# Feeding x transposed and applying its norm afterwards, in a one-core encoder block

## The chip, the cores and the metric

One core of a Trainium2 chip. The metric is the device time of one launch in microseconds (us), as the median of several runs; a separate profiled execution leaves a trace. PE is TensorE, DVE is VectorE, ACT is ScalarE, POOL is GpSimd, and SP is the engine whose queue issues nearly all loads.

## The reference

One layer over S = 256 tokens and D = 1024 channels. Cut to what matters here:

```python
xn = rms_norm(x, norm1_g)             # x * rsqrt(mean(x*x) + eps) * g, a factor per token and a gain per channel
a_x, a_g, b_q, ..., d_g, gate_logits = split(xn @ w_in)
y_a = rglru(a_x, a_g, ...)            # conv over time, gates, a linear recurrence both ways, times gelu(a_g)
y_b = diff_attention(b_q, b_k, b_v)
y_c = mla(c_q, c_kv, c_kpe)
y_d = retention(d_q, d_k, d_v, d_g)   # head layer norm of the result, times silu(d_g)
gates = sigmoid(gate_logits + gate_b)
merged = sum(gates[i] * (y_i @ w_br_i))
x = x + merged @ w_out
...                                   # feed-forward and a gated projection
```

Since rms_norm's factor is one number per token, `xn @ w` is the same as `(x * g) @ w` with each token's row multiplied by its factor.

## The kernel before

Every matrix product is made of three: weights and activations are split into a rounded part `hi` and a rest `lo`, and hi*hi, hi*lo and lo*hi are added in PSUM. `split` and `pieces` do this: ACT copies to `hi` (line 196), DVE subtracts for `lo` (line 190). For the pieces counted in `V_HI` with an even number, DVE makes `hi` too. Weights arrive in loads of up to 1 MB (`load`, line 372, three buffers `raw`), in the order in which they are used. `b_mode` (weights stationary, 256 columns out, one chunk = one load = 48 products) serves the recurrence branch and its gate; `a_mode` (activations stationary, up to 512 columns) the rest.

At the start x comes in as rows (four loads), each row tile's factor is computed (`rstd`: ACT's Square with a sum, a Sqrt, DVE's reciprocal), DVE multiplies, PE transposes 16 tiles, and `split_scaled` (lines 220 and 221) writes `xT` in hi and lo with the gain. Then four chunks `a_in(u)` follow, each evicted by a convolution of four taps on ACT and DVE (tile `xc`). `derived_params` runs behind the first: small parameter work, mostly DVE (`rg`, `lamp`, `spt`, `sp`).

Beside this main stream of products, generators do the branches' inner work: `a_mix` (the recurrence), `b_rot` and `b_mix` (attention), `c_mix`, `d_rot` and `d_mix`. `start` puts one on a list, and `tick`, called behind each chunk, lets it advance by a credit. A scheduler then lays out each engine's instructions in one fixed order; `tc.high_priority` moves some ahead. Each engine runs its list in order, so one that waits holds up what is behind it. The tile names in the trace: `raw` loaded weights, `hi` and `lo` their parts, `acc` and `mm` PSUM banks, `xs` x (later the merged sum), `par` the small parameters, `bd` the recurrence's gate weights, `bT` the attention's queries and keys, `y` the branches' results.

Of the kernel before, what the change touches and what calls it, by code (L numbers as in the profile page):

```python
# [26 lines left out]

V_HI = range(8, 40)

# [129 lines left out]
def _pack(w):  # L159
    import numpy as np  # L160

    return {'x': np.asarray(w['x']), 'weights': _pack_weights(w), 'params': _pack_params(w), 'lru': _pack_lru(w),
            'pT': np.ascontiguousarray(np.asarray(w['p'])[0, 0].T.reshape(2, P, S).transpose(1, 0, 2)),
            'gate_b': np.ascontiguousarray(np.asarray(w['gate_b'])[0]), 'decay': _decay()}


@with_exitstack
def encoder_kernel(ctx: ExitStack, tc: tile.TileContext, a, out):
# [55 lines left out]

    xs = const.tile([P, 2, D], F32, name="xs")
    par = const.tile([P, N_PAR], F32, name="par")
    with tc.high_priority(FIRST):
        for t in range(2):
            for c in range(2):
                w = slice(512 * c, 512 * c + 512)  # L230
                nc.sync.dma_start(xs[:, t, w], a['x'][0, t * P:(t + 1) * P, w])  # L231
        nc.sync.dma_start(par[:, :O_LATE], a['params'][:, :O_LATE])

# [5 lines left out]

    act(eps[:, 2:3], eps[:, 0:1], AF.Sqrt)  # L240
    nhalf = const.tile([P, 16], F32, name="nhalf")
# [5 lines left out]
    rope = par[:, O_ROPE:].rearrange("p (t w) -> p t w", t=2)  # L247
    rg = const.tile([P, 2, 2, 2, 80], F32, name="rg")
    lams = const.tile([P, 4], F32, name="lams")
# [4 lines left out]

    def derived_params():
        nc.sync.dma_start(par[:, O_LATE:], a['params'][:, O_LATE:])
# [8 lines left out]
        lamp = const.tile([P, 2, 64], F32, name="lamp")  # L265
        tt(lamp, lv[:, :, 0, :], lv[:, :, 1, :], MULT)
# [3 lines left out]

        nc.vector.tensor_scalar(out=gng, in0=c1('ret_gn_g'), scalar1=0.5, scalar2=None, op0=MULT)
        nc.vector.tensor_scalar(out=subg, in0=c1('diff_sub_g'), scalar1=1.0 - LAM_INIT, scalar2=None, op0=MULT)


        lamc = par[:, _COL['lru_lambda']:_COL['lru_lambda'] + 16]
        spt = const.tile([P, 4, 16], F32, name="spt")
        y_, s_, z_, q_ = (spt[:, j, :] for j in range(4))
# [151 lines left out]
    def b_mode(xh, xl, name, n0):  # L429

        ps = acc_bank().rearrange("p (f s) -> p f s", s=S)
        raw = load(name, 0, n0)
        for f in range(2):
            hi, lo = pieces(raw, f * 1024, 1024)
            for k in range(8):
                w = slice(k * P, (k + 1) * P)
                mm(ps[:, f, :], hi[:, w], xh(k), k == 0, False)
                mm(ps[:, f, :], hi[:, w], xl(k), False, False)
                mm(ps[:, f, :], lo[:, w], xh(k), False, k == 7)
        tick(1)  # L440
        return ps

    def b_wide(name, n0):
# [12 lines left out]
        return ps  # L456

    W_in = 'w_in'
    xh = lambda k: xTh[:, k, :]
    xl = lambda k: xTl[:, k, :]  # L460

    with tc.tile_pool(name="br", bufs=1) as br:
# [4 lines left out]
        def SH(name):  # L467
            return br.tile([P, 512], F32, tag="SH", name=name, bufs=NS)

        with tc.high_priority(FIRST):  # L470
            for t in range(2):
                r_ = rstd(xs[:, t, :], lambda: SH("xsq"))
                nc.vector.tensor_scalar(out=xs[:, t, :], in0=xs[:, t, :], scalar1=r_, scalar2=None, op0=MULT)
            for k2 in range(4):
                pt = mm_bank().rearrange("p (k s) -> p k s", s=S)
                for t in range(2):
                    for k in range(2):
                        kk = 2 * k2 + k
                        transpose(pt[:, k, t * P:(t + 1) * P], xs[:, t, kk * P:(kk + 1) * P])
                for k in range(2):  # L480
                    kk = 2 * k2 + k
                    split_scaled(xTh[:, kk, :], xTl[:, kk, :], pt[:, k, :], c1('norm1_g', kk))

# [242 lines left out]
        def c_in():  # L726

            cs = [L("cs").rearrange("p (t c) -> p t c", t=2) for _ in range(3)]
            for c0, n0, nn in ((0, O_CQ, 384), (384, O_CKV, 320)):
                ps = a_full(xh, xl, W_in, 8, n0, nn)  # L730
                for t in range(2):
                    for lo in range(0, 704, 256):
                        u0, u1 = max(lo, c0), min(lo + 256, c0 + nn)
                        if u0 < u1:
                            act(cs[lo // 256][:, t, u0 - lo:u1 - lo], ps[t][:, u0 - c0:u1 - c0], AF.Copy)
            return cs
# [135 lines left out]
        def d_in():  # L872

            res = [[], []]
            for j, o0 in enumerate((O_DQ, O_DK)):
                ps = a_full(xh, xl, W_in, 8, o0, 512)
                for c in range(2):
                    x = SH("dx").rearrange("p (t c) -> p t c", t=2)
                    for t in range(2):
                        act(x[:, t, :], ps[t][:, 256 * c:256 * c + 256], AF.Copy)  # L880
                    dst = [L("dqk", F32R).rearrange("p (h s) -> p h s", s=S) for _ in range(2)]
# [16 lines left out]
        def d_vg(c):  # L898
# [3 lines left out]
            for p in range(2):  # L902
                v = L("dv").rearrange("p (t c) -> p t c", t=2)
                for t in range(2):
                    act(v[:, t], ps[t][:, 256 * p:256 * p + 256], AF.Copy)
                pairs[p].append(v.rearrange("p t (h e) -> p t h e", e=P))
            ps = a_full(xh, xl, W_in, 8, O_DG + 512 * c, 512)
            for p in range(2):
                sg = L("dsg").rearrange("p (t c) -> p t c", t=2)
                for t in range(2):  # L910
                    pv = ps[t][:, 256 * p:256 * p + 256]
                    act(sg[:, t], pv, AF.Tanh, scale=0.5)
                    stt(sg[:, t], sg[:, t], 1.0, pv, ADD, MULT)
# [3 lines left out]
        def d_mix(p, qT, kT, v, sg, yy):  # L917
# [51 lines left out]
        for u in range(4):  # L969
            xc = a_in(u)  # L970
            if u == 0:
                derived_params()
# [159 lines left out]
```

## Time and profile before

| | |
|---|---|
| median of 3 runs | 727.56 us (726.92 to 728.64) |
| profiled execution | 728.43 us, of which the span of the trace is 726.6 us |
| PE busy | 711.9 us of the span |
| DVE, ACT, POOL busy | 535.9, 437.9 and 47.1 us |
| loads | 128.45 MB, 177 GB/s over the span |

A row of the timeline gives start, length, engine, line, operation and tiles (written `out<-in`); the brackets at its end give the idle time ahead of it and who ended that. In a row of waits stand the total, the number and the longest. A busy PE is not PE at its peak; the pace of its products is read from the starts.

### The profile page before, as it was taken

How to read it: one execution, taken by the hardware profiler on the slowest of the kernel's cores; microseconds unless marked ns; L12 is line 12 of the kernel's file. 1: busy time of each engine (PE TensorE's matmuls, PEld its weight loads, DVE VectorE, ACT ScalarE, POOL GpSimd, SP SyncE). 2: the span in 40 equal slices, each digit the busy share in tenths (PEclk: the TensorE clock that was granted, in tenths of full speed). 3: DMA queues.
4: the chain of work that ended last, by engine and by line, in shares of the span. 5: the costliest groups of instructions: out<-in, count | busy, mean ns of one | idle time of the engine just before them, and what ended most of it. 6: DMA issues, size and time to landing. Idle time of an engine off the chain costs nothing.

```text
span 726.6 us, 10163 instructions
## 1 busy us (share of the span) xinstructions
PE 711.9 (98%) x3810; PEld 607.6 (84%) x3810; DVE 535.9 (74%) x931; ACT 437.9 (60%) x770; POOL 47.1 (6%) x58
## 2 busy tenths in 40 slices
PE   5999999999999999999999999999999999999997
PEld 4988889998888888888888888888888888888876
DVE  5988978888777878967667588776788887445652
ACT  7589858585755994765655434545855555445551
POOL 0000003212011022200000012000000000000000
PEclk9999999999999999999999999999999999999999
DMA  8754554365344256355436583554565455536611
GB/s 304 261 225 169 179 174 142 117 222 214 133 162 137 93 175 230 120 186 175 138 125 233 199 281 126 179 197 144 182 223 176 174 182 203 195 124 233 230 57 53
DMA packets 22801, 128.45 MB, mean 177 GB/s; under 512 B 2656, under 2 KB 2912, under 8 KB 9440
## 3 DMA queue, kind: packets, MB, share of 16 engines
q1 hardware_dynamic: 22752, 127.80, 49.9%
q8 instruction: 30, 0.49, 0.3%
q14 instruction: 19, 0.16, 0.1%
HBM read 126.74 MB, written 1.05 MB: 176 GB/s over the span
## 4 chain that ended last, share of the span: by engine, by line
PE 88%; DVE 5%; ACT 2%; DMA 2%; POOL 1%; issue 1%; SPq 0%; ACTq 0%; DVEq 0%
PE acc L199 66%; PE acc L203 12%; PE mm L199 5%; PE mm L212 3%; DVE lo L190 2%; DMA raw<-in_weights_dram 2%; PE mm L203 1%; ACT hi L196 1%; ACT be L196 1%; DVE bsm L675 0%; DVE xT L193 0%; POOL bss L296 0%; POOL crq L296 0%; POOL crk L296 0%; SPq L231 0%
## 5 line engine op out<-in xcount | busy, mean ns | idle before, releaser
L190 DVE TENSOR_TENSOR lo<-raw,hi 128x1024 fp32r<-128x1024 f32 (+3 forms) x226 | 268.5, 1194 | 104.0 <-ACT hi L196 103.4
L196 ACT ACTIVATE hi<-raw 128x1024 fp32r<-128x1024 f32 (+3 forms) x210 | 217.1, 1040 | 194.0 <-PE acc L199 148.0
L199 PE MATMUL acc<-hi,xT 128*128 128x512 f32 (+3 forms) x752 | 233.4, 385 | 0.0
L199 PEld LDWEIGHTS acc<-hi,xT 128*128 128x128 f32 x752 | 139.5, 188 | 25.9
L199 PE MATMUL acc<-hi,y 128*128 128x512 f32 x448 | 142.7, 393 | 0.0
L199 PE MATMUL acc<-lo,xT 128*128 128x512 f32 (+3 forms) x376 | 142.6, 379 | 0.0
L199 PEld LDWEIGHTS acc<-hi,y 128*128 128x128 f32 x448 | 84.1, 188 | 18.0 <-ACT y L196 0.3
L203 PE MATMUL acc<-xT,hi 128*128 128x512 f32 x256 | 90.4, 399 | 0.0
L199 PE MATMUL acc<-lo,y 128*128 128x512 f32 x224 | 87.4, 391 | 0.0
L199 PEld LDWEIGHTS acc<-lo,xT 128*128 128x128 f32 x376 | 70.8, 188 | 12.1
L203 PE MATMUL acc<-xT,lo 128*128 128x256 f32 x256 | 71.6, 281 | 0.0
L203 PEld LDWEIGHTS acc<-xT,hi 128*128 128x128 f32 x256 | 48.1, 188 | 12.1
L199 PEld LDWEIGHTS acc<-lo,y 128*128 128x128 f32 x224 | 42.1, 188 | 8.2
L203 PEld LDWEIGHTS acc<-xT,lo 128*128 128x128 f32 x256 | 48.4, 189 | 0.1
L199 PE MATMUL acc<-xT,hi 128*128 128x256 f32 x256 | 47.7, 287 | 0.4 <-ACT xT L196 0.2
L199 PEld LDWEIGHTS acc<-xT,hi 128*128 128x128 f32 x256 | 40.4, 193 | 1.0 <-DVE xT L193 0.6
L199 PE MATMUL acc<-hi,h 128*128 128x512 f32 x128 | 40.8, 398 | 0.0
L199 PE MATMUL acc<-xT,lo 128*128 128x256 f32 x128 | 36.2, 284 | 0.3 <-DVE lo L190 0.3
L199 PEld LDWEIGHTS acc<-hi,h 128*128 128x128 f32 x128 | 24.0, 188 | 5.7
L199 PE MATMUL acc<-lo,h 128*128 128x512 f32 x64 | 25.3, 396 | 0.0
L199 PEld LDWEIGHTS acc<-xT,lo 128*128 128x128 f32 x128 | 24.5, 192 | 0.6 <-DVE lo L190 0.6
L199 PE MATMUL acc<-hi,cT 128*128 128x384 f32 (+1 forms) x80 | 24.2, 369 | 0.3 <-ACT cqp L196 0.3
(224 smaller groups left out, 896.2 us busy)
## 6 DMA issues: line engine op xcount, KB each, us to landing
raw<-in_weights_dram SPq DMA_DIRECT2D x104, 1024.0 KB, 4.8
raw<-in_weights_dram SPq DMA_DIRECT2D x6, 512.0 KB, 3.5
raw<-in_weights_dram SPq DMA_DIRECT2D x4, 576.0 KB, 3.8
bd<-in_lru_dram SPq DMA_DIRECT2D x8, 256.0 KB, 5.3
gb<-in_gate_b_dram SPq DMA_DIRECT2D x8, 256.0 KB, 5.3
dec<-in_decay_dram SPq DMA_DIRECT2D x8, 256.0 KB, 6.2
raw<-in_weights_dram SPq DMA_DIRECT2D x2, 768.0 KB, 4.5
raw<-in_weights_dram SPq DMA_DIRECT2D x2, 640.0 KB, 3.6
```

The source lines that it names most:

```text
L190: nc.vector.tensor_tensor(out=o, in0=x, in1=y, op=op)
L196: nc.scalar.activation(o, x, f, **kw)
L199: nc.tensor.matmul(o, lhsT=lhsT, rhs=rhs, start=start, stop=stop)
L203: nc.tensor.matmul(o, lhsT=lhsT, rhs=rhs, start=start, stop=stop, skip_group_check=True)
L212: nc.tensor.transpose(o, x, ident[:x.shape[0], :x.shape[0]])
```

## The change

x is given a second time, transposed and with norm1's gain in front (`xT`), and loaded in four parts, each followed by a quarter of the first chunk's weights in runs of 1 KB. `x_split` scales by the gain and splits straight from the loaded data, unnormalized. The rows of x are loaded behind the third chunk's weights (`xr`) and used only for the tokens' factors: `x_stats` gives `rc` (a factor per token, tokens on partitions), its half `rch`, and `rT` (the same along the free dimension, through two small products). Who reads a product applies the factor: DVE multiplies by `rT` for the recurrence branch (tiles `xa` and `gel`), ACT's copies take `rc` as their scale, the gates' addition becomes a multiply and add, and retention's values get it behind their norm on POOL. The first chunk has an order of its own in `b_mode`, and loads of the first three chunks are issued first. Eight products of zeros open PE's list. `rg` and two small scalings go from DVE to POOL. `V_HI` is narrower. `a_mix` of the first three chunks is started behind the third chunk.

```diff
-V_HI = range(8, 40)
+V_HI = range(16, 32)
+WARM = 8
...
+    with tc.high_priority(2 * FIRST):
+        nc.scalar.dma_start(par[:, 8:O_LATE], a['params'][:, 8:O_LATE])
+        for u in range(3):
...
+            if u:
+                nc.sync.dma_start(raw, src.rearrange("(p c) -> p c", c=2048))
+                continue
...
+            for k in range(0, 8, 2):
+                o0, o1 = 8 + S * k if k else 0, 8 + S * (k + 2)
+                nc.sync.dma_start(xs_[:, o0:o1], a['xT'][:, o0:o1])
+                w = slice(P * k, P * (k + 2))
+                nc.sync.dma_start(raw0v[:, :, w], src[:, :, w])
...
+        for _ in range(WARM):
+            mm(pt[:, 0:P], cold, cold, True, True)
...
-                    tt(rg[:, j, cs, :, o:o + w], rope[:, :, r0:r0 + w], g, MULT)
+                    nc.gpsimd.tensor_tensor(out=rg[:, j, cs, :, o:o + w], in0=rope[:, :, r0:r0 + w], in1=g, op=MULT)
...
+                    with tc.high_priority(FIRST):
+                        if k0 + k2 == 0:
+                            nc.vector.tensor_copy(out=hv[:, :, w], in_=rw)
+                        else:
+                            act(hv[:, :, w], rw, AF.Copy)
+                        x_split(k0 + k2)
+                        tt(lv[:, :, w], rw, hv[:, :, w].bitcast(F32), SUB)
+                        x_split(k0 + k2 + 1)
...
+    def x_split(k):
+        split_scaled(xTh[:, k, :], xTl[:, k, :], xin[:, k, :], xs_[:, k:k + 1])
+
+    def x_stats():
+        st = small.tile([P, 2, 2], F32, tag="xst", name="xst", bufs=1)
+        for t in range(2):
+            for c in range(2):
+                act(xr[2 * t + c], xr[2 * t + c], AF.Square, accum_out=st[:, t, c:c + 1])
+        tt(rc, st[:, :, 0], st[:, :, 1], ADD)
+        act(rc, rc, AF.Sqrt, scale=1.0 / D, bias=eps[:, 0:1])
+        nc.vector.reciprocal(rc, rc)
+        nc.vector.tensor_scalar(out=rch, in0=rc, scalar1=0.5, scalar2=None, op0=MULT)
+        pr = mm_bank()
+        for t in range(2):
+            mm(pr[:, t * P:(t + 1) * P], rc[:, t:t + 1].to_broadcast([P, P]), ident, True, True)
+        act(rT, pr[:, :S], AF.Copy)
...
-                tt(g, ps, gb, ADD)
+                stt(g, ps, rc[:, t:t + 1], gb, MULT, ADD)
...
-            ps = b_mode(xh, xl, W_in, O_AX + u * 256)
+            pp = b_mode(xh, xl, W_in, O_AX + u * 256)
+            if u == 0:
+                x_stats()
+            ps = SH("xa").rearrange("p (f s) -> p f s", s=S)
+            tt(ps, pp, rT.unsqueeze(1).to_broadcast([P, 2, S]), MULT)
...
-            act(gel, ps, AF.Gelu_apprx_tanh)
+            tt(gel, ps, rT.unsqueeze(1).to_broadcast([P, 2, S]), MULT)
+            act(gel, gel, AF.Gelu_apprx_tanh)
...
-                        act(x[:, t, :], ps[t][:, 256 * p:256 * p + 256], AF.Copy)
+                        act(x[:, t, :], ps[t][:, 256 * p:256 * p + 256], AF.Copy, scale=rc[:, t:t + 1])
...
             rsqrt(mv[:, :, :, 1], 1.0, EPS, e2(2))
+            nc.gpsimd.tensor_tensor(out=mv[:, :, :, 1], in0=mv[:, :, :, 1],
+                                    in1=rc.unsqueeze(2).to_broadcast([P, 2, 2]), op=MULT)
...
-            ga.append(start(a_mix(u, xc, ha[u])))
+            ga.append(a_mix(u, xc, ha[u]))
+            for g in ([], [], ga[:3], ga[3:])[u]:
+                start(g)
```

What SP issues at the start of the program, before (`xs` is x, `raw` weights, `par` parameters, `bd` gate weights of the recurrence):

```order
L231 DMA xs<-in_x_dram 128x512 x4
L232 DMA par<-in_params_dram 128x107
L372 DMA raw<-in_weights_dram 128x2048 x2
L256 DMA par<-in_params_dram 128x1168
L372 DMA raw<-in_weights_dram 128x2048
L543 DMA bd<-in_lru_dram 128x512 x2
```

And in the changed kernel:

```order
L257 DMA xs<-in_xT_dram 128x512
L259 DMA raw<-in_weights_dram 128x2x256
L251 DMA raw<-in_weights_dram 128x2048 x2
L556 DMA xr<-in_x_dram 128x512 x4
L289 DMA par<-in_params_dram 128x1168
L405 DMA raw<-in_weights_dram 128x2048 x4
L621 DMA bd<-in_lru_dram 128x512 x6
```

The first two of these rows come four times in turn; x's rows now stand behind three chunks of weights, the late parameters behind them, and the recurrence's gate weights behind the seventh load.

DVE around the evictions of the first chunks, before. The `lo` in the middle is the first half of the third chunk (u=2), the last one its second half:

```order
L190 TENSOR_TENSOR lamp<-par 128x128
L280 TENSOR_SCALAR spt<-spt 128x16
L190 TENSOR_TENSOR lo<-raw,hi 128x1024
L193 SCALAR_TENSOR_TENSOR xc<-acc,par,xc 128x254
L267 TENSOR_REDUCE lams<-lamp 128x2
L193 SCALAR_TENSOR_TENSOR xc<-acc,par,xc 128x255
L193 SCALAR_TENSOR_TENSOR lams<-lams 128x1
L281 RECIPROCAL spt<-spt 128x16
L193 SCALAR_TENSOR_TENSOR xc<-acc,par,xc 128x255
L190 TENSOR_TENSOR spt<-spt 128x16
L190 TENSOR_TENSOR lo<-raw,hi 128x1024
```

And in the changed kernel. The `lo` row at the top is both halves of the second and third chunk:

```order
L202 TENSOR_TENSOR lo<-raw,hi 128x1024 x4
L202 TENSOR_TENSOR rc<-xst 128x2
L532 RECIPROCAL rc<-rc 128x2
L533 TENSOR_SCALAR rch<-rc 128x2
L202 TENSOR_TENSOR xa<-acc,rT 128x512
L202 TENSOR_TENSOR lamp<-par 128x128
L202 TENSOR_TENSOR xa<-acc,rT 128x512
L205 SCALAR_TENSOR_TENSOR xc<-xa,par,xc 128x254 x2
L205 SCALAR_TENSOR_TENSOR xc<-xa,par,xc 128x255 x4
L300 TENSOR_REDUCE lams<-lamp 128x2
L313 TENSOR_SCALAR spt<-spt 128x16
L205 SCALAR_TENSOR_TENSOR xc<-xa,par,xc 128x254
```

Behind the last row come three more taps of `xc` and six small instructions on `lams` and `spt`, and then the first `lo` of the fourth chunk (u=3): it moved from among the taps to behind the factors, two `xa`, and ten taps.

ACT at the start of its list before (`xsq` is a square that is only summed, `nst` the sums and factors):

```order
L196 ACTIVATE eps<-eps 128x1
L196 ACTIVATE xsq,nst<-xs 128x512 x3
L196 ACTIVATE nst<-nst,eps 128x1
L196 ACTIVATE xsq,nst<-xs 128x512
L196 ACTIVATE nst<-nst,eps 128x1
L196 ACTIVATE xT<-mm,par 128x256
L196 ACTIVATE hi<-raw 128x1024
```

And in the changed kernel, from the first full `hi` on (`xst` holds the sums of squares):

```order
L208 ACTIVATE hi<-raw 128x1024 x3
L208 ACTIVATE xr,xst<-xr 128x512
L208 ACTIVATE hi<-raw 128x1024
L208 ACTIVATE xr,xst<-xr 128x512 x3
L208 ACTIVATE rc<-rc,eps 128x2
L208 ACTIVATE rT<-mm 128x256
L208 ACTIVATE spt<-par 128x16
L208 ACTIVATE xc<-xa,par 128x256 x2
L208 ACT_TABLE_LOAD
L208 ACTIVATE spt<-spt 128x16
```

The squares, which opened ACT's list before, now stand among the splits of the third chunk. On PE the two products for `rT` stand five products into the third chunk. Later, the generators' products stand behind the main stream's by more than before: the attention's last scores come 30 `acc` products later, and the second merge, which reads their results, stands where it stood.

More of the change, by code (lines that the diff above doesn't have):

```diff
@@ L160, in _pack, with _pack_x @@
     import numpy as np
-    return {'x': np.asarray(w['x']), 'weights': _pack_weights(w), 'params': _pack_params(w), 'lru': _pack_lru(w),
+    return {'x': np.asarray(w['x']),
+            'xT': _pack_x(w),
+            'weights': _pack_weights(w), 'params': _pack_params(w), 'lru': _pack_lru(w),
             'pT': np.ascontiguousarray(np.asarray(w['p'])[0, 0].T.reshape(2, P, S).transpose(1, 0, 2)),
             'gate_b': np.ascontiguousarray(np.asarray(w['gate_b'])[0]), 'decay': _decay()}
+def _pack_x(w):
+    import numpy as np
+    g = np.asarray(w['norm1_g'][0]).reshape(8, P).T
+    return np.concatenate([g, np.asarray(w['x'])[0].T.reshape(8, P, S).transpose(1, 0, 2).reshape(P, 8 * S)], axis=1)
 @with_exitstack
@@ L221, in split_scaled @@
         stt(lo, src, col, hi.bitcast(F32), MULT, SUB)
-    xs = const.tile([P, 2, D], F32, name="xs")
+    xs_ = const.tile([P, 8 + 2 * D], F32, name="xs")
+    xs = xs_[:, 8:].rearrange("p (t d) -> p t d", t=2)
+    xin = xs_[:, 8:].rearrange("p (k s) -> p k s", s=S)
     par = const.tile([P, N_PAR], F32, name="par")
[L227 to L232, printed above, removed]
+    rg = const.tile([P, 2, 2, 2, 80], F32, name="rg")
+    early = {}
+    with tc.high_priority(2 * FIRST):
+        nc.scalar.dma_start(par[:, 8:O_LATE], a['params'][:, 8:O_LATE])
+        for u in range(3):
+            o = _offsets()[0]['w_in', 0, O_AX + 256 * u][0]
+            src = a['weights'][o:o + 1024 * 256]
+            raw = early[O_AX + 256 * u] = raws.tile([P, 2048], F32, tag="raw", name="raw", bufs=3)
+            if u:
+                nc.sync.dma_start(raw, src.rearrange("(p c) -> p c", c=2048))
+                continue
+            raw0v = raw.rearrange("p (f c) -> p f c", f=2)
+            src = src.rearrange("(p f c) -> p f c", f=2, c=1024)
+            for k in range(0, 8, 2):
[3 more added lines that the diff above has]
+                nc.sync.dma_start(raw0v[:, :, w], src[:, :, w])
+        cold = rg.rearrange("p a b c w -> p (a b c w)")[:, :P]
+        nc.vector.memset(cold, 0.0)
+        pt = mm_bank()
+        for _ in range(WARM):
+            mm(pt[:, 0:P], cold, cold, True, True)
     ident = near.tile([P, P], F32, name="ident")
@@ L431, in b_mode @@
         ps = acc_bank().rearrange("p (f s) -> p f s", s=S)
-        raw = load(name, 0, n0)
+        if (name, n0) == ('w_in', O_AX):
+            for k0 in (0, 4):
+                hi = ring.tile([P, 1024], F32R, tag="hi", name="hi", bufs=NR)
+                lo = ring.tile([P, 1024], F32R, tag="lo", name="lo", bufs=NR)
+                hv, lv = (v.rearrange("p (f c) -> p f c", f=2) for v in (hi, lo))
+                for k2 in (0, 2):
+                    w = slice(P * k2, P * k2 + 2 * P)
+                    rw = raw0v[:, :, P * (k0 + k2):P * (k0 + k2) + 2 * P]
+                    with tc.high_priority(FIRST):
+                        if k0 + k2 == 0:
[5 more added lines that the diff above has]
+                        x_split(k0 + k2 + 1)
+                    for k in (k2, k2 + 1):
+                        w = slice(k * P, (k + 1) * P)
+                        for f in range(2):
+                            mmg(ps[:, f, :], hv[:, f, w], xh(k0 + k), k0 + k + f == 0, False)
+                            mmg(ps[:, f, :], hv[:, f, w], xl(k0 + k), False, False)
+                            mmg(ps[:, f, :], lv[:, f, w], xh(k0 + k), False, k0 + k == 7)
+            tick(1)
+            return ps
+        raw = early[n0] if name == W_in and n0 in early else load(name, 0, n0)
         for f in range(2):
@@ L456, in b_wide @@
         return ps
+    rc = const.tile([P, 2], F32, name="rc")
+    rch = const.tile([P, 2], F32, name="rch")
+    rT = const.tile([P, S], F32, name="rT")
+    def x_split(k):
[13 more added lines that the diff above has]
+        act(rT, pr[:, :S], AF.Copy)
     W_in = 'w_in'
@@ L468, in SH @@
             return br.tile([P, 512], F32, tag="SH", name=name, bufs=NS)
+        xr = [SH("xr") for _ in range(4)]
         with tc.high_priority(FIRST):
[L471 to L482, printed above, removed]
+            for j in range(4):
+                w = slice(512 * (j % 2), 512 * (j % 2) + 512)
+                nc.sync.dma_start(xr[j], a['x'][0, (j // 2) * P:(j // 2 + 1) * P, w])
         def y4():
```

24 lines of the change are left out of this document (12 added, 12 removed).

## Prediction

> **What bounds the kernel now.** I read the engines' totals first, then who waited for whom on TensorE (PE), then the chain that ended last in order of time, and last the start of the trace row by row.
>
> ```profile
> span 726.6 us, 10163 instructions
> PE 711.9 (98%) x3810; PEld 607.6 (84%) x3810; DVE 535.9 (74%) x931; ACT 437.9 (60%) x770; POOL 47.1 (6%) x58
> ```
> ```profile
> PE mm L212 <- DVE xs L473: 8.0, 2, 7.3
> PE mm L203 <- DVE ckn L193: 0.5, 1, 0.5
> ```
> ```profile
> 3.03 7.26 DMA raw<-in_weights_dram
> 10.32 1.07 ACT hi L196
> 11.41 1.23 DVE lo L190
> 14.74 16.58 PE acc L199 x134
> 31.32 1.73 PE mm L199 x8
> 33.05 5.75 PE acc L199 x48
> ...
> 274.51 0.66 DVE y L193
> ...
> 460.10 21.79 PE acc L199 x96
> ```
> PE is busy 98% of the span and waits 8.0 us at the start; its next longest wait is 0.5 us. So the time is the start plus PE's own work, and the change must be priced by when PE gets going. A convenient mark is the start of the fourth chunk of weights (u=3): each chunk is 48 products of 256 columns, 5.75 us when nothing is missing (row at 33.05), and the 134 products that end at 31.32 are the end of the third. **The mark before is 31.3 us.** Everything PE does behind it is the same in both kernels, so what the mark moves the end moves, unless a new wait takes it back.
>
> **When the loads land.** SP's issues, and the time from each issue to its landing:
> ```profile
> 0.72 1.79 SPq L231 DMA_DIRECT2D xs<-in_x_dram  x4
> 2.56 0.43 SPq L232 DMA_DIRECT2D par<-in_params_dram  x1
> 3.03 0.91 SPq L372 DMA_DIRECT2D raw<-in_weights_dram  x2
> 4.52 0.44 SPq L372 DMA_DIRECT2D raw<-in_weights_dram  x1
> 5.01 1.66 SPq L543 DMA_DIRECT2D bd<-in_lru_dram  x2
> ```
> ```profile
> DMA to landing us min/median/max: 2.6/3.5/4.3
> par<-in_params_dram SPq DMA_DIRECT2D x1, 53.5 KB, 4.0
> raw<-in_weights_dram SPq DMA_DIRECT2D x1, 1024.0 KB, 9.3
> raw<-in_weights_dram SPq DMA_DIRECT2D x1, 1024.0 KB, 12.2
> bd<-in_lru_dram SPq DMA_DIRECT2D x1, 256.0 KB, 12.4
> ```
> The first row of the second fence is of the four pieces of x (first landing 0.72+2.6 = 3.3, last 2.08+4.3 = 6.4); par lands at 6.6, the first weights at 10.3, the second (issued at about 3.5) at 12.8, the third at 16.7, the first bd at 17.4. They land in the order of issue: 1.0 us for each 256 KB of x, 2.5 us for 1 MB of weights in 8 KB runs, 0.7 us for 256 KB in 2 KB runs, 0.2 us for 128 runs of 428 B.
>
> After the change the second weights still stand behind the same 3.2 MB (x, the small parameters, two chunks). What differs is that the first chunk is cut into 1024 runs of 1 KB. No row has such runs. By bytes they cost what they cost now, 0 more. By count they cost 8 x 0.7 = 5.6 instead of 2.5, 3.1 more. Between par's 0.2 for 128 runs of 428 B and bd's 0.7 for 128 of 2 KB a straight line gives 0.39 at 1 KB: 3.1 us, 0.6 more, and I take that. Call the landing of the second weights W: **W = 12.8 + 0.6 = 13.4** (12.8 to 15.9); the third lands at W+2.5.
>
> The Trainium skill (DMA: Bandwidth & Descriptors, Specifications) puts the smallest transfer that runs at line rate at 512 B. By it the 1 KB runs cost nothing extra, W is 12.8 and the sum below comes out 0.6 us lower; this trace has 2 KB runs near the full rate and nothing between.
>
> **Chunks 0 to 2.** x's transpose (16 PE instructions), the two rstd chains and the PSUM evictions leave the front. The first pair of x and weights lands at about 4.5, then a pair every 1.8 to 2.0, and ACT and DVE need less for a pair (two x splits and half a weight split each, about 1.6). So chunk 0 is done about 3 us after its last piece (W-2.5), before chunk 1 has its weights; its own start, early as it is, decides nothing. Chunk 1 needs hi and lo as chunk 0 does now: 10.3 to 12.64, so W+2.35, and runs from W+2.1 in effect (two products precede the first lo). Chunk 2 starts at W+7.85; with two small products for rT, **chunk 3 could start at W+14.0 = 27.4, its first lo due at W+14.25.**
>
> **The new wait.** DVE's order puts chunk 3's first lo behind everything that needs rT (the tokens' factors). That chain, by rows of ACT and DVE at the start:
> ```profile
> 4.61 0.63 ACT L196 ACTIVATE xsq<-xs 128x512 f32<-128x512 f32 x1 [0.51 <-DMA xs<-in_x_dram]
> 5.27 0.63 ACT L196 ACTIVATE xsq<-xs 128x512 f32<-128x512 f32 x1
> 6.42 0.64 ACT L196 ACTIVATE xsq<-xs 128x512 f32<-128x512 f32 x1 [0.23 <-DMA xs<-in_x_dram]
> 7.70 0.16 DVE L314 RECIPROCAL nst<-nst 128x1 f32<-128x1 f32 x1 [0.24 <-ACT nst L196]
> 9.43 0.47 ACT L196 ACTIVATE xT<-mm,par 128x256 fp32r<-128x256 f32 x1 [1.76 <-PE mm L212]
> 18.31 2.00 ACT L196 ACTIVATE hi<-raw 128x1024 fp32r<-128x1024 f32 x2
> ```
> ```profile
> 24.71 0.48 DVE L193 SCALAR_TENSOR_TENSOR xc<-acc,par,xc 128x255 f32<-128x255 f32 x1
> 25.10 0.17 DVE L284 TENSOR_SCALAR spt<-spt 128x16 f32<-128x16 f32 x1
> 25.18 1.23 DVE L190 TENSOR_TENSOR lo<-raw,hi 128x1024 fp32r<-128x1024 f32 x1
> 34.66 0.69 DVE L190 TENSOR_TENSOR ii<-ii,xc 128x512 f32<-128x512 f32 x1
> 35.26 0.49 DVE L193 SCALAR_TENSOR_TENSOR xc<-acc,par,xc 128x254 f32<-128x254 f32 x1
> ```
> ACT: from W+2.5 a hi (1.0), a square (0.66, start to start at 4.61 and 5.27), a hi (1.0), two squares; the fourth square starts at W+6.5. x's rows come behind the third weights at 0.7 to 1.0 us each, so the fourth is there in time. From the last square's start to the end of the reciprocal took 6.42 to 7.86 = 1.4: W+7.9. PE reaches the two products, five into chunk 2, at W+8.45; 0.45 for them, 0.5 for the copy: **rT at W+9.45**.
> DVE then, start to start: two xa at 0.60, lamp 0.3, ten conv taps at 0.39, a reduce and a reciprocal 0.4, six small ones at 0.085: 6.3; then lo 1.23. **Chunk 3's lo is ready at W+17.0, 2.8 us after PE wants it.** The mark is W+16.8 = 30.2 against 31.3: **1.1 us gained**, where the earlier loads alone would give 3.9. Behind it the second half's lo comes 1.8 later and is due 2.9 later, so the wait is paid once.
>
> **The other parts.**
> ```profile
> 25.00:50.00 25.00, 25.00 (x161) 23.12 (x160) 23.98 (x51) 17.64 (x30) 0.00 (x0) 1.00 0.66 232
> 50.00:100.00 50.00, 50.00 (x223) 41.58 (x222) 41.75 (x53) 42.07 (x79) 0.00 (x0) 1.00 0.52 179
> ```
> (Columns: PE, weight loads, DVE, ACT, POOL.) xa and gel add eight DVE products of 0.69 (5.5 us); the narrower V_HI takes eight casts from DVE and gives ACT eight hi of 1.06 (8.5 us). The recurrence, two chunks later, moves DVE work out of the 25 to 50 stretch, where DVE is full, into 50 to 100, where it has 8 us free and ACT as much: 0 on PE. Scales in ACT copies ride along at 0. SP issues six transfers more (four xr, three more for the split chunk, one parameter load gone to ACT's queue, where ACT is idle until 3.37); the xr MB delays the fourth weights to about W+9.3 = 22.7, wanted by ACT at 27: covered by 4 us. rg's products move to POOL, 6% busy. POOL's extra product in d_mix delays it by about 1 us before a stretch of 21.8 us of PE work (row at 460.10): 0, and 1 us each if that were gone. The warm-up products stand before any data: 0. The raw x squares write into tiles nobody waits for.
>
> Sum: 728.43 - 1.1 = 727.3 for the profiled execution, which lies 0.9 above the median of the three runs; on the median **727.56 - 1.1 = 726.4**. A measurement here tells about 0.2%, 1.5 us, from no change.
>
> **Rivals.** *B: no wait at chunk 3* (0.27). If the statistics are there 2.8 us sooner, the mark is W+14.0: 723.6, and 723.0 with W = 12.8. For it: the wait rests on 20 durations added up, and DVE's work alone from chunk 1's lo to chunk 3's would just fit. Against: x's rows are last in the queue and ACT's two hi stand among the squares.
> ```profile
> 8.71 3.25 PE L212 MATMUL mm<-ident,xs 128*128 128x128 f32 x14 [0.78 <-DVE xs L473]
> 116.32 0.44 PE mm L212 x4
> ```
> Transposes cost 0.22 us each at the start and 0.11 later: PE begins at half pace. If it stays so for all of chunk 0 (48 x 0.24 = 11.5 from about 5), chunk 1 starts at 16.5 to 17 instead of 15.5, which the forecast hides in its wait and B does not: then B is 724.7. The Trainium skill (TensorE: Matmul & The Clock Gate, Part 1) has the full clock granted after about 3.4 us of sustained work; the rows agree in size, and whether eight warm-up products and a gap count, no row shows.
>
> *C: attention late at the second merge* (0.13, no change).
> ```profile
> 243.54 0.97 PE L199 MATMUL mm<-bT 64*128 64x256 f32 x9 [0.43 <-ACT be L196]
> 249.57 3.40 PE acc L199 x18
> 271.87 0.48 PE L199 MATMUL acc<-hi,y 128*128 128x512 f32 x1
> 278.22 0.48 PE L199 MATMUL acc<-hi,y 128*128 128x512 f32 x1
> ```
> The last scores end at 244.5, the last y is split at 275.2 (chain), and the merge takes it as its seventh and eighth k, 2.7 us after 278.22: 5.7 us to spare. In the new order the last scores stand 30 acc products later, 5.9 us by the row at 249.57 (18 with the weights' wait in 3.4) and 12 wider ones at 0.23: 0.2 us late, and each us that the chain is longer costs one. It eats the gain from 1 us on: 726.6 to 728.5.
>
> *D: runs are paid by count, at the early pace* (0.15, slower). If 128 runs cost the 1.0 us that x's 128 runs of 2 KB cost, the first chunk's 1024 take 8 instead of 3.7 (6.6 to 10.3): W = 17.1, the mark 33.9, 2.6 lost: 730.1. It decides from W = 16 on. Against it: par's 128 runs took 0.2.
>
> **Numbers.** The forecast has 0.45, 725.4 to 727.6 by itself; about half of it lies beyond 0.2%. Faster 0.22+0.27 = 0.49, same 0.23+0.13+0.01 = 0.37, slower 0.14. The range runs from B with the cheapest W, less 0.4 for one of the later waits, to D's middle: 722.6 to 729.4.
>
> **What would show it.** PE's first weight products at about 5 us; the second weights landing at 13.4; an idle stretch of PE of 2 to 3 us at 27 to 30, released by DVE's lo, with ACT's rT copy ending near 22.9; the fourth chunk beginning near 30.2; the same 0.5 us waits near 240 to 285. Without the idle stretch it is B; with the second weights at 16 or later, D; with a new PE wait for y near 275, C. I am wrong altogether if PE waits somewhere between 35 and 230.

## The result, and the profile after

The changed kernel takes 731.64 us (median of 5 runs, 730.16 to 735.83), the kernel before 726.92 on the same chip (726.52 to 728.64). The ratio is 1.0078, with a 95% interval of 1.0060 to 1.0097: it is **slower by 0.8%**, where 726.4 and a range of 722.6 to 729.4 were forecast. (The ratio is taken over all runs; the two medians alone give 1.0065.) The same kernel run again beside another set of the kernel before gave 1.0072 (1.0053 to 1.0091). Two traces of it are used below: the first, of an execution of 735.83 us, the slowest of its five, and a second, of 732.01.

The totals of the first:

```profile
span 734.1 us, 10185 instructions
PE 718.4 (98%) x3814; PEld 613.6 (84%) x3814; DVE 535.4 (73%) x922; ACT 452.7 (62%) x779; POOL 48.2 (7%) x72
```

DVE has as much work as before (535.9), ACT 14.8 us more, and PE is busy 6.5 us longer with about as many instructions, some of them at a lower clock. The start, as the chain that ended last:

```profile
5.58 8.84 DMA raw<-in_weights_dram
...
14.44 1.07 ACT hi L208
...
23.66 0.40 ACT rT L208
...
25.92 1.28 ACT L208
...
29.36 2.00 ACT hi L208 x2
...
31.40 8.76 PE acc L211 x59
```

The second weights land at 14.42, rT is there at 24.06, and PE's third product behind the third chunk starts at 31.40. Two products precede it, 0.24 us, so the mark is 31.16 where it was 31.32: of the forecast gain of 1.1 us, 0.2 is left in this execution. The third product is not the one that the forecast has there:

```profile
31.40 0.50 PE L211 MATMUL acc<-hi,xT 128*128 128x512 f32 x1 [1.39 <-ACT hi L208]
31.74 0.28 PE L211 MATMUL acc<-xT,lo 128*128 128x256 f32 x1
```
```profile
30.24 1.21 DVE L202 TENSOR_TENSOR lo<-raw,hi 128x1024 fp32r<-128x1024 f32 x1
```

It has 512 columns, so it belongs to a later load that `a_mode` reads; it stands ahead in PE's order and waits for that load's hi on ACT. The fourth chunk's own first lo is ready at the same time, about 31.4, and its product follows at 31.74 without a gap. The waits of PE (total, times, longest):

```profile
PE acc L211 <- ACT hi L208: 2.5, 3, 1.4
PE mm L224 <- DVE bx L202: 2.2, 2, 1.6
PE mm L224 <- DVE xs L205: 1.5, 1, 1.5
...
PE mm L224 <- DVE by L202: 1.1, 1, 1.1
```

The first row is mostly the new wait at the fourth chunk, which the forecast had. The second was not there before and was not forecast: PE waits for the attention's rotated heads `bx` until 150.2 and 152.2 us, where in the kernel before PE is busy without a gap. This is what the prediction called wrong altogether: PE waits between 35 and 230. The third, at 702 us, comes and goes with the execution: the second trace has none of it. The last is near the second merge, at 280.

Busy time of PE, weight loads, DVE, ACT and POOL, then PE's clock, from 110 to 150 us. First the kernel before with one part of the stretch, then the changed one with three:

```profile
110.00:150.00 40.00, 40.00 (x294) 38.58 (x294) 35.48 (x65) 28.80 (x51) 13.65 (x10) 1.00 0.43 149
110.00:120.00 10.00, 10.00 (x61) 8.87 (x60) 7.93 (x15) 9.97 (x20) 0.00 (x0) 1.00 0.46 162
```
```profile
110.00:150.00 40.00, 38.65 (x277) 37.25 (x275) 32.13 (x54) 35.70 (x55) 10.26 (x8) 1.00 0.36 126
110.00:120.00 10.00, 10.00 (x61) 8.95 (x60) 3.94 (x6) 9.97 (x22) 0.00 (x0) 1.00 0.38 122
130.00:140.00 10.00, 10.00 (x85) 10.00 (x84) 9.93 (x14) 8.83 (x13) 1.38 (x1) 1.00 0.19 67
140.00:150.00 10.00, 8.65 (x52) 8.30 (x50) 8.47 (x20) 7.14 (x11) 4.34 (x4) 1.00 0.47 170
```

ACT has 6.9 us more to do here. From 110 to 120 it is full in both kernels, but DVE, which needs its results, is busy 3.94 of 10 where it was 7.93; from 130 to 140 DVE is full, 9.93, and late. What ACT does more, by groups from 105 to 150 us, before and after:

```profile
L196 ACT ACTIVATE hi<-raw 128x1024 fp32r<-128x1024 f32 (+2 forms) x13 | 11.6, 892 | 2.7 <-PE acc L199 2.7
L196 ACT ACT_TABLE_LOAD x3 | 3.8, 1283 | 0.1
```
```profile
L208 ACT ACTIVATE hi<-raw 128x1024 fp32r<-128x1024 f32 (+2 forms) x16 | 14.4, 922 | 3.3 <-PE acc L211 2.5 <-ACT bsq L208 0.8
L208 ACT ACT_TABLE_LOAD x5 | 6.4, 1283 | 0.1
```

Three casts more and two table loads more; the kernel before with the narrower V_HI alone has as many (experiment 4: 16 and 5). Sigmoids of the recurrence still run at 110.2 to 111.8 us, where the kernel before ends its last at 106.3, and the exponentials behind them need a load of 1.28. The chain of the changed kernel through the stretch shows a way by which that reaches PE:

```profile
111.84 1.28 ACT L208
113.13 0.91 ACT aa L208 x2
...
127.36 0.68 DVE brs L720
...
143.01 1.64 POOL brs L329
...
147.36 0.69 DVE bx L202
...
152.19 0.96 PE mm L224 x4
```

The wait is not all. Behind it the products of 320 columns are slow (start, length):

```profile
150.24 0.66 PE L224 MATMUL mm<-ident,bx 128*128 128x128 f32 x4 [1.59 <-DVE bx L202]
...
152.19 0.96 PE L224 MATMUL mm<-ident,bx 128*128 128x128 f32 x4 [0.56 <-DVE bx L202]
...
153.48 0.47 PE L211 MATMUL acc<-lo,xT 128*128 128x320 f32 x1
...
155.85 0.31 PE L211 MATMUL acc<-lo,xT 128*128 128x320 f32 x1
```

From about 152.4 to 155.8 a product takes 0.47 instead of 0.31 us, start to start 0.27 instead of 0.15; the clock granted from 150 to 160 us is 0.83. By an estimate from that, 3.4 us at half clock add 1.7 us to 2.2 us of waiting.

### The profile page after: what moved, and what is told of

It reads as the page before. It is cut to its first block, busy times and chain, and to the rows that moved or that the text cites. A ratio compares the mean times of both kernels' runs of the same rounds, so it can differ in the third digit from the quotient of the medians.

```text
span 734.1 us, 10185 instructions
## 1 busy us (share of the span) xinstructions
PE 718.4 (98%) x3814; PEld 613.6 (84%) x3814; DVE 535.4 (73%) x922; ACT 452.7 (62%) x779; POOL 48.2 (7%) x72
## 4 chain that ended last, share of the span: by engine, by line
PE 85%; DVE 6%; ACT 4%; DMA 2%; issue 1%; POOL 1%; SPq 1%; ACTq 0%; DVEq 0%
PE acc L211 63%; PE acc L215 12%; PE mm L211 6%; PE mm L224 4%; DMA raw<-in_weights_dram 2%; DVE lo L202 2%; ACT hi L208 1%; PE mm L215 1%; POOL brs L329 0%; DVE gel L202 0%; DVE y L202 0%; ACT L208 0%; DVE bsm L754 0%; ACT rr L208 0%; ACT be L208 0%
## 5 line engine op out<-in xcount | busy, mean ns | idle before, releaser
L202 DVE TENSOR_TENSOR lo<-raw,hi 128x1024 fp32r<-128x1024 f32 (+4 forms) x228 | 268.3, 1183 | 113.7 <-ACT hi L208 112.9
L208 ACT ACTIVATE hi<-raw 128x1024 fp32r<-128x1024 f32 (+4 forms) x219 | 224.4, 1033 | 188.4 <-PE acc L211 134.2
L215 PE MATMUL acc<-xT,hi 128*128 128x512 f32 (+1 forms) x288 | 98.8, 395 | 1.3 <-DVE hi L476 1.3
L215 PE MATMUL acc<-xT,lo 128*128 128x256 f32 x272 | 77.4, 286 | 0.1
L215 PEld LDWEIGHTS acc<-xT,hi 128*128 128x128 f32 x288 | 55.2, 197 | 13.7 <-ACT xT L208 1.6
L215 PEld LDWEIGHTS acc<-xT,lo 128*128 128x128 f32 x272 | 52.6, 193 | 0.6 <-DVE lo L202 0.4
L211 PE MATMUL acc<-xT,hi 128*128 128x256 f32 x224 | 40.9, 284 | 1.1 <-ACT hi L208 1.1
L211 PEld LDWEIGHTS acc<-xT,hi 128*128 128x128 f32 x224 | 34.9, 192 | 1.6 <-ACT hi L208 1.5
L211 PE MATMUL acc<-xT,lo 128*128 128x256 f32 x112 | 31.9, 285 | 0.8 <-DVE lo L202 0.8
```

The lines of the kernel that those rows point to most:

```text
L202: nc.vector.tensor_tensor(out=o, in0=x, in1=y, op=op)
L208: nc.scalar.activation(o, x, f, **kw)
L211: nc.tensor.matmul(o, lhsT=lhsT, rhs=rhs, start=start, stop=stop)
L215: nc.tensor.matmul(o, lhsT=lhsT, rhs=rhs, start=start, stop=stop, skip_group_check=True)
```

## The experiments

Four theories at the beginning. R: the recurrence, two chunks later, fills ACT and DVE where the attention's heads are prepared. V: the narrower V_HI does it through ACT's casts. G: DVE's added products with rT do it. Against all of them, that the start's gain gets lost on its way to the end. All ratios are to runs of the kernel before on the same chip, 5 rounds, with 95% intervals.

**1. Recurrence at once, in the changed kernel.**
```diff
-            ga.append(a_mix(u, xc, ha[u]))
-            for g in ([], [], ga[:3], ga[3:])[u]:
-                start(g)
+            ga.append(start(a_mix(u, xc, ha[u])))
```


> The changed kernel with one edit: each block's recurrence starts with its chunk, as in the kernel before; all else of the change stays. Theory R (the recurrence, two chunks later, fills ACT and DVE at 105 to 145 us and makes the rotated heads bx late): PE's 1.8 us wait for bx at 148 us and the 0.83 clock of 150 to 160 us are gone, the wait of 2.5 us at chunk 3 stays, and the time is the kernel before's less what the start gained, 0.2 to 0.4 us, so 726 to 727.5. Theory V (the narrower V_HI gives ACT too many casts in the same stretch): still 730 to 732, with the wait for bx. Theory G (DVE's eight more products for xa and gel): 730 to 732 as well.

Measured: 726.75 us, 0.9992 (0.9981 to 1.0003). The wait for bx is gone, and the clock stays at 1.00. Of 0.78% lost this one part gives back 0.86%. ACT's casts and table loads do not go with the wait: from 105 to 150 us this trace has the same 16 and 5 as the changed kernel, and ACT is about as busy (35.12 against 35.70):
```profile
110.00:150.00 40.00, 39.96 (x296) 38.39 (x295) 37.20 (x64) 35.12 (x53) 9.83 (x9) 1.00 0.44 152
```
What differs is the place of the work. The first transposes of the heads, in the kernel before and in the changed one:
```profile
116.16 0.60 PE L212 MATMUL mm<-ident,bx 128*128 128x128 f32 x4
```
```profile
133.50 0.60 PE L224 MATMUL mm<-ident,bx 128*128 128x128 f32 x4
```
Here they start at 114.7, and at 132.9 to 134.2 in every trace with the recurrence two chunks later. So with the late recurrence the heads' work begins late as well, 17 us in the changed kernel.

**2. V_HI as before, in the changed kernel** (`V_HI = range(6, 38)`).


> The changed kernel with one edit: V_HI is range(6, 38), the chunks that DVE casts in the kernel before (the changed kernel begins two counts earlier), so DVE takes eight casts back from ACT. Theory R: no help, 730 to 732, PE still waits for bx near 148 us. Theory V: 726 to 727.5, no wait for bx. Theory G: DVE has eight casts more, so 732 or over.

Measured: 732.43 us, 1.0060 (1.0040 to 1.0080), wait for bx 1.4 us. The casts alone are not the cause. Nor does a full ACT have to be: with 13 casts and 3 table loads it is busy 31.6 of the 40 us from 110 to 150 here, less than in experiment 1, and PE waits.

**3. The kernel before with its recurrence two chunks later.**
```diff
-            ga.append(start(a_mix(u, xc, ha[u])))
+            ga.append(a_mix(u, xc, ha[u]))
+            for g in ([], [], ga[:3], ga[3:])[u]:
+                start(g)
```


> The kernel before with one edit: its recurrence two chunks later, as the changed kernel has it. Theory R: slower than the kernel before by 3 to 5 us, 730 to 732, with a wait of PE for bx near 150 us that the kernel before does not have. Theory V and theory G: no change, 726 to 728, since the cast table and the products are those of before.

Measured: 728.94 us, 1.0023 (1.0011 to 1.0034): slower, but by 1.7 us, not 3 to 5, and without a wait for bx. It waits 1.0 us for by near 275, as every trace with the recurrence two chunks later does (1.0 to 1.1) and none with it at once. So R costs something by itself, and most of what it costs in the changed kernel needs a companion.

**4. The kernel before with the narrower V_HI** (`range(18, 34)`).


> The kernel before with one edit: V_HI is range(18, 34), the chunks that DVE casts in the changed kernel, so eight casts of 1.06 us more on ACT and eight fewer on DVE. Theory V: 730 to 732, PE waits for bx near 150 us. Theory R and theory G: no change, 726 to 728.

Measured: 728.18 us, 1.0014 (1.0002 to 1.0026), no wait for bx.

**5. The kernel before with both.**


> The kernel before with two edits: recurrence two chunks later, and V_HI range(18, 34). Alone the first cost 1.7 us and the second 1.0. If the two are all that the changed kernel loses by (theory R with V), they have to make its wait for bx near 148 us here: 731 to 732. If DVE's added products are needed for that wait (theory G: eight of 0.69 us for the tokens' factors, four of them on the branch's second half just before the rotated heads), the two costs only add up: 729.5 to 730.5, and no wait for bx.

Measured: 732.78 us, 1.0061 (1.0049 to 1.0073), wait for bx 1.5 us. Together they cost more than the 0.37% of their sum, and the wait appears without any product of the change. G is not needed.

**6. The changed kernel without the product of gel with rT.** gelu reads PSUM; the tokens' factors are left out there.


> The changed kernel without the product of the branch's second half with rT: gelu reads PSUM itself, as before, so the tokens' factors are left out there and four DVE products of 0.69 us with them. Theory G with R: PE's wait for bx at 148 us is gone or under 0.5 us, and the time is that of the late recurrence in the kernel before, 728.5 to 729.5. If the late recurrence alone makes that wait: 730.5 to 732.

Measured: 733.05 us, 1.0071 (1.0058 to 1.0084), bx waited for 2.2 us. G falls as the cause, as far as these go: taking four of its eight products away changes nothing. The four of xa stay in every run of the changed kernel.

**7. Both loads off, the recurrence late** (V_HI as before, no gel product).


> The changed kernel, recurrence two chunks later, with both other loads off: V_HI range(6, 38) and no product with rT in the branch's second half (its factors left out). Theory (the late recurrence uses up the reserve of ACT and DVE at 105 to 145 us, and either load alone is then enough to make bx late by 1.5 us): as the kernel before with its recurrence late, 728.3 to 729.5, no wait for bx over 0.5 us. If bx is late here as well, the late recurrence needs neither, and something else of the change does it (the earlier start, xa): 730.5 to 732.5.

Measured: 730.70 us, 1.0045 (1.0028 to 1.0063); bx waited for 0.5 us. Without the two loads the wait shrinks to 0.5 us, from 1.4 without the casts alone (2) and 2.2 without gel's products alone (6), as the theory of the used up reserve has it. The time missed its 728.3 to 729.5 by over 1 us and lies in the other expectation's range. The trace, like others below, has a stretch at low clock behind the fourth chunk's wait, which neither expectation had.

**8. bx ahead on DVE and ACT, the recurrence late.** Norm and rotation of the heads under `tc.high_priority(300)`.


> The changed kernel, recurrence two chunks later, with one edit: the heads' norms and rotations (brs, rope, bx) get a priority that puts them ahead of the recurrence's products and of weight splits on DVE and ACT. PE's order stays. Theory queue (bx waits behind the recurrence's work on DVE and ACT): PE's wait for bx at 148 us falls below 0.3 us, and the time comes down by 2 to 3 us against the changed kernel, to 1.003 of the kernel before or less. Theory place (the attention blocks now stand too late on PE, and their later chains run into the second merge): the wait for bx goes, the waits for by at 278 us and behind it stay, and no more than 1.5 us comes back.

Measured: 738.24 us, 1.0149 (1.0128 to 1.0170): neither. The wait for bx is gone, and another took its place, with the low clock behind it:
```profile
PE acc L211 <- DVE lo L202: 3.1, 1, 3.1
```
```profile
140.00:150.00 10.00, 6.86 (x32) 6.45 (x31) 8.19 (x19) 3.46 (x6) 1.86 (x2) 0.83 0.29 88
```
Moving the heads ahead swaps one wait for another. Whether all the work before 150 us would fit, the run does not tell: DVE is busy 8.19 of these 10 us, and ahead of the late lo it stands idle twice for POOL's part of the heads' norm, which the edit put in front of that lo:
```profile
139.47 0.69 DVE L202 TENSOR_TENSOR bx<-bx,brs 128x512 f32<-128x512 f32 x1 [1.25 <-POOL brs L329]
141.98 0.69 DVE L202 TENSOR_TENSOR bx<-bx,brs 128x512 f32<-128x512 f32 x1 [1.81 <-POOL brs L329]
```
So this order is a bad one. One with the lo between the two was not tried.

**9. One chunk later instead of two** (`([], ga[:2], ga[2:3], ga[3:])[u]`).


> The changed kernel with the recurrence one chunk later instead of two. At once is 0.999, two later is 1.008. If the cost grows with each chunk of delay: 1.002 to 1.005. If it comes only where ACT and DVE have no reserve left: 0.999 to 1.001, and no wait for bx.

Measured: 732.27 us, 1.0068 (1.0052 to 1.0083). Both expectations missed: one chunk costs as much as two. Its trace has three shorter waits for bx (2.2 us together) and 1.6 for ckn, and the heads' first transposes start at 125.8. Why the first chunk of delay costs nearly all is open.

**10. The changed kernel again.**


> The changed kernel as it is, for a second profile and more runs on the chip of the others. If the half clock of 152 to 156 us follows from the wait for bx, it is there again, PE's lost time in 140 to 160 us is again over 4 us, and the ratio is again near 1.008. If it fell on that one run by chance, the second profile has the wait (1.7 us) without the half clock, and the ratio over more runs is 1.004 to 1.006.

Measured: 731.89 us, 1.0072 (1.0053 to 1.0091). The same wait for bx (1.59 and 0.56 us), this time at full clock. The low clock fell elsewhere, behind the other new wait, at the fourth chunk. From 30 to 35 us, first trace and second:
```profile
30.00:35.00 5.00, 3.61 (x30) 3.56 (x30) 5.00 (x13) 3.80 (x5) 0.00 (x0) 1.00 0.20 28
```
```profile
30.00:35.00 5.00, 4.48 (x24) 4.44 (x25) 5.00 (x13) 2.54 (x4) 0.00 (x0) 0.68 0.24 87
```
In the second PE is busy 0.9 us longer and does 24 products for 30. So the drop does not belong to the wait for bx, as the first expectation had it, and it is no single accident that the median leaves out, as the second had it (1.004 to 1.006): it changes its place.

**11. The wait at the fourth chunk taken out, the recurrence late.** The split of that chunk's weights gets the priority of the first loads, so hi and lo stand ahead of the taps and the softplus.
```diff
-            hi, lo = pieces(raw, f * 1024, 1024)
+            hi, lo = pieces(raw, f * 1024, 1024, ahead=FIRST if n0 == O_AX + 768 else AHEAD_S)
```


> The changed kernel, recurrence still two chunks later, with the split of the fourth chunk's weights ahead of the softplus and tap work on DVE: the forecast's wait of 2.8 us (2.5 in the trace) without its cause. Theory: the wait falls below 0.6 us and the mark comes 2 us earlier, but with the late recurrence bx is not earlier by as much, so PE's wait for it near 148 us grows from 1.8 to 3 or more and the time stays at 730 to 732. Rival: the start's gain passes through, 729 to 730.

Measured: 729.83 us, 1.0030 (1.0018 to 1.0042). The wait fell to 0.7 us, the wait for bx stayed at 2.2 and did not grow, and by the ratios 0.4% to 0.5% came back: the rival held, and what is taken out at the start passes even with the late recurrence. How much of it is the wait and how much the low clock that can follow it is not shown: in the one trace the second weights land at 14.48 and from 15 to 25 us the clock is 0.82 to 0.84, so its mark is hardly earlier.

**12. Where the start's gain goes with the recurrence at once.** In experiment 1 PE is 1.5 us ahead of the kernel before at 40 us (by the start of the same product), 0.8 at 254 us and 0.5 at its end. Its waits and its chain near 283 us:
```profile
PE mm L215 <- DVE ckn L205: 1.3, 1, 1.3
```
```profile
282.57 1.22 DVE lo L202
283.79 0.67 DVE ckn L205
284.50 2.48 PE mm L215 x23
```
The kernel before waits 0.5 us for ckn, and its row of PE there starts at 284.52. The two start the keys' products at the same time, although PE comes earlier in one, since the chain to ckn runs from 274.5 us on through DVE and POOL alone, with a weight split of 1.2 us in front. The edit puts the split of the keys into `tc.high_priority(AHEAD_S)`.


> The changed kernel with the recurrence at once and one more edit: the split of the normalized keys (ckn) at the priority of the loads, so that it stands ahead of a weight split of 1.2 us on DVE. Theory: with the recurrence at once the start gains 1.5 to 2 us, and PE's wait for ckn at 283 us, 1.3 us there and 0.5 before, takes most of it back. Then this edit gives 0.8 to 1.3 us: 725.4 to 726.0, the wait under 0.5. Rival: the wait moves to cpe or to the second keys right behind, 726.5 to 727.

Measured: 724.62 us, 0.9951 (0.9939 to 0.9964), no wait for ckn. It gave 0.4% where 0.1% to 0.2% were expected.

**13. par behind the first chunk on SP's queue.**


> As the kernel with the early keys, and the first parameter load stands on SP's queue behind the first chunk of weights, not on ACT's at the start. Theory: two queues at the start made the first piece of x land 1.3 us later than before (4.62 against 3.35). Then the first piece lands at 3.3 to 3.6, the second weights at 13.2 to 13.6 instead of 14.3, and, as the later wait is shorter, 0.6 to 1 us of it reaches the end: 724.5 to 725.2. Rival: the 1 KB runs or the rows of 2080 bytes are the cause; the first piece lands at 4.4 to 4.6 again and the time is the other kernel's within 0.4.

Measured: 726.08 us, 0.9969 (0.9958 to 0.9980). The first piece of x landed at 3.84 (4.3 to 5.0 with par on the other queue), but the second weights only at 14.15, and the time is not lower. The first half of the theory holds; the second gets no support, though one trace says little beside a spread of W of 1.3 us (next section).

**14. The fourth chunk's split ahead, with 12.**


> The kernel with the recurrence at once and the early keys, and the split of the fourth chunk's weights ahead of the softplus and tap work on DVE. Theory: with the recurrence at once PE still waits 1.1 us for that chunk's second lo at 32.4 us; the edit takes 0.8 to 1.1 us out there and all of it reaches the end: 723.4 to 724.0 where the early keys alone gave 724.6. Rival: what DVE puts off (taps, softplus) makes the first recurrence late, and PE or the attention waits for that instead: 724.5 to 726.

Measured: **723.06 us, 0.9940 (0.9924 to 0.9957)**, the fastest of all, and faster than both kernels. PE's waits after the first weights:
```profile
PE acc L211 <- DVE lo L202: 0.8, 1, 0.8
PE mm L211 <- ACT be L208: 0.8, 2, 0.5
PE mm L211 <- DMA bd<-in_lru_dram: 0.5, 1, 0.5
PE mm L224 <- DVE xs L205: 0.5, 1, 0.5
```
Nothing over 0.8 us is left, the fourth chunk is not waited for (the 0.8 for lo is the second chunk's), and the clock stays at 1.00 at the places of the drops. The time lies in the theory's direction, but 0.1% below experiment 12's is inside both intervals.

**15. The first chunk in runs of 2 KB, with 14.**


> As the kernel with the fourth chunk's split ahead, and the first chunk is packed so that each of its four pieces has runs of 2 KB instead of two of 1 KB. If the 1 KB runs cost what the forecast's straight line gave them (0.6 us), the second weights land at 12.7 to 13.4 instead of 13.3 to 14.4, and the time is 0.3 to 0.7 lower, 723.0 to 723.6. If the length of the runs costs nothing and the early pace of the queue is what is slow: 13.3 to 14.4 again and the same time within 0.4.

Measured: 724.21 us, 0.9950 (0.9935 to 0.9965), the second weights at 13.18. That is the early end of the other traces' spread (13.19 to 14.51, next section), and the time is not lower: no gain from longer runs is seen.

**16. V_HI as before, with 14.**


> The kernel with the recurrence at once, early keys and the fourth chunk's split ahead, and V_HI range(6, 38), so eight casts go from ACT back to DVE. Alone on the kernel before the narrow table cost 0.14%. If that is so here: 722 to 723, 0.992 to 0.993 of the kernel before. If the table matters only beside the late recurrence: as without it, 0.994, within 0.001. If DVE is the fuller engine with the changed kernel's products on it: 0.996 and over.

Measured: 725.07 us, 0.9968 (0.9954 to 0.9981). This is the third expectation's range: the narrower table is no loss once the recurrence starts at once. Whether it gains is not settled, since in that trace the second weights landed at 14.51, 1.3 later than in experiment 14's.

## Why the prediction was wrong, point by point

**The failed step** is the sentence on the recurrence: "moves DVE work out of the 25 to 50 stretch, where DVE is full, into 50 to 100, where it has 8 us free and ACT as much: 0 on PE". It weighed the stretch to which the first of the work goes. The last of it is past 100: the recurrence's last two scans run on DVE at 118.4 and 124.4 us in the kernel before and at 125.2 and 132.3 in the changed one. The sum leaves that stretch out, and there ACT and DVE prepare the attention's heads, whose own work begins 17 us later too (experiment 1). In place of 0 the runs show 0.23% for the move alone (3), 0.61% with the narrower V_HI (5), and all of the loss in the changed kernel (1). That V_HI "gives ACT eight hi of 1.06" was priced at 0 by the same look at 25 to 100; alone it costs 0.14% (4). The added products of DVE, also priced at 0: leaving out four of the eight gained nothing (6).

**W.** 13.4 was forecast, and 14.42 seen in the first trace. Over the twelve traces with these loads it lies between 13.19 and 14.51, median 13.6: the forecast was good, and the spread of 1.3 us between executions, as large as the gain, was missing from it. The kernel before has such a spread as well: with its loads W is 11.62 to 12.78 in four traces, and the forecast started from the latest. The straight line's 0.6 for the short runs is not borne out: where nothing holds them up, pieces of 256 KB land 0.7 us apart with runs of 1 KB and of 2 KB (15). That W is later all the same has another cause, which stays open. Rival D, runs paid by count, is out.

**The wait at the fourth chunk.** rT was forecast at W+9.45 and came at W+9.64; the first lo at W+17.0 and came at W+16.95; the mark at W+16.8, and it is at W+16.74 in the first trace. The second trace has its landing at 13.52 and the third product at 30.52, the same distance. Its cause was half described. DVE's order behind rT makes lo late as forecast, and in experiments 2 and 7 PE waits 1.5 us for it. But ACT's hi stand behind rT too, behind four steps of the taps and a table load of 1.28 at 25.92, in the chain above: in the changed kernel hi ends both waits, 0.74 and 1.39 us. With hi and lo moved ahead the wait falls to 0.7 (11) or goes (14). And "the wait is paid once" holds for the lo, but not for the time: a stretch at low clock can follow, some 1.7 us, and in the second trace this undoes the earlier start altogether.

**The rivals.** B (no wait, 723.6) did not happen, but its size was right: with the split ahead, the recurrence at once and the later waits out of the way (14), PE is 3.8 us ahead of the kernel before at 40 us, where the earlier loads alone were to give 3.9, and the kernel takes 723.1. C had a real place and the wrong part in it: PE waits 1.1 us for by near the second merge in the changed kernel, as in experiment 3. It was given 0.13 and priced at 728.5 at most; as one of several late chains it adds to the loss. That rotated heads, 130 us earlier, could be late for the same reason, was not asked, though C's own argument (the attention's blocks stand later, their chain is as long) led there.

**What is not settled.** Experiments 1, 3 and 5 show which parts lose together. What makes bx late is argued from the traces and not shown by a run of its own: the sum of the work on ACT and DVE before 150 us, or the later place of the heads' work; 8 does not part the two. How the loss of some 5 us divides is not shown: by the first trace 2.2 us of waits for bx, 1.7 at low clock, 1.5 for xs near the end, 1.1 for by, less 0.2 at the start, and smaller waits; the second trace has the low clock elsewhere and no wait for xs. Why one chunk of delay costs as much as two (9), and the rest of experiment 7, stay open.

## What to carry to other kernels

When work is moved later, follow its last piece and not its first: price the stretch in which it ends, with that stretch's rows for every engine it uses, and name who else must be ready by then. An engine's free time over the whole kernel, or in a neighbouring stretch, says nothing about it. And where an early gain is expected at the end, look for the next chain that runs beside the gained work, here ckn at 283 us, since it can take back what the rest gained; with the recurrence at once, freeing it gave 0.4%, and the start's own fix 0.1%.

## What the runs showed of the hardware that was not expected

**PE's clock falls after short waits.** The waits at the fourth chunk, 0.74 and 1.39 us within 2.7 us, were followed by some 3.4 us at half clock in the second trace. Of the six traces with those two waits of 0.7 and 1.4 to 1.5 us (the two of the changed kernel, experiments 2, 6, 7 and 8) four have a clock of 0.66 to 0.68 from 30 to 35 us. In all others it is 1.00 there, and the kernel before has no fall in its whole span up to its last product.

The clock's own record in the traces shows what parts the four from the two. Every low stretch within a kernel lasts 3.41 us, and where a trace has several, their starts lie whole multiples of that apart: 7.90 and 31.79 us in the second trace, seven times 3.413. So there is a fixed grid of windows, placed differently in each execution. Two windows in a row at the fourth chunk in the first trace, and two in the second:
```profile
26.09:29.51 3.42, 2.68 (x23) 2.48 (x22) 3.42 (x13) 3.41 (x7) 0.00 (x0) 1.00 0.12 48
29.51:32.92 3.41, 2.02 (x13) 1.77 (x14) 3.41 (x10) 3.41 (x4) 0.00 (x0) 1.00 0.01 2
```
```profile
28.38:31.79 3.41, 1.77 (x11) 1.52 (x12) 3.41 (x11) 3.41 (x5) 0.00 (x0) 1.00 0.01 2
31.79:35.21 3.42, 3.42 (x18) 3.42 (x17) 3.42 (x9) 0.95 (x2) 0.00 (x0) 0.50 0.40 153
```
In the first the two waits fall into two windows, 0.74 and 1.39 us idle, and the clock stays. In the second one window has most of both, PE is idle 1.64 of its 3.41 us, and the next window has half the clock. So it is in all six: 1.64 to 2.17 us idle in one window where the clock falls, at most 1.49 where it does not. At the wait for bx 1.83 us in one window brought a fall (first trace), and 1.60 or less brought none in six others. Idle time is not the whole rule, since three other falls (experiments 8, 9 and 11, at 255, 251 and 18 us) follow windows with 1.4, 0.6 and 1.5 us of it.

The Trainium skill (TensorE: Matmul & The Clock Gate, Part 1) describes a free-running window of about 3.4 us whose activity sets the clock. The grid, and its placing by execution, agree with that; the Trainium skill's advice to avoid gaps of over about 3 us (Why this matters for your kernels) is too lenient here, where the longest gap ahead of five of the falls was 1.4 to 1.6.

**The loads' start varies.** In the traces one or more of the first pieces of 256 KB, now this one and now that, land 1.0 to 2.3 us after the one before, where others take 0.7, which makes the spread of W. It is so with runs of 1 and of 2 KB, and in the one trace with par on SP's queue.

**The feed-forward runs at one of two paces.** From 550 to 600 us a hi product of 512 columns takes 399 or 391 to 394 ns, whichever kernel it is (the kernel before and the second trace of the changed one):
```profile
L203 PE MATMUL acc<-xT,hi 128*128 128x512 f32 x143 | 50.6, 399 | 0.0
```
```profile
L215 PE MATMUL acc<-xT,hi 128*128 128x512 f32 x145 | 50.3, 391 | 0.0
```
It does 145 for 143 in the same time. Over the whole stage the same products take 88.9 us in nine of the eighteen traces and 87.4 in the other nine. This alone moves single executions by 1.5 us, and is one more reason to compare medians here and not two traces' spans.
